# A channel mixer by block products with seven multiplications for eight, in two phases with the rows between them in DRAM

## The chip, the cores and the metric

The kernel runs on one core of one Trainium2 chip. Its engines work side by side and meet through semaphores: TensorE (PE) multiplies matrices, VectorE (DVE), ScalarE (ACT) and GpSimd (POOL) do elementwise work, SyncE (SP) issues the DMAs. The metric is the device time of one execution in microseconds; lower is better.

## The reference, cut to what matters

One layer of a hybrid backbone works on 1152 tokens of width 1024: 128 prompt tokens and 1024 latent ones. A mixer of DeltaNet and retention heads comes first, then the channel mixer, which is what the change is about:

```
h = layer_norm(x) * (1.0 + sc2) + sh2
f = einsum('btf,fd->btd', square(relu(einsum('btd,df->btf', h, w_ff1) + b_ff1)), w_ff2) + b_ff2
x = layer_norm(ALPHA * x + g2 * f, ln2_w, ln2_b)
```

`w_ff1` is 1024 x 4096, `w_ff2` 4096 x 1024, all in float32.

## The kernel before, in words

Every large product is made of three matmuls for one: a float32 operand is split into a high part, rounded to the format that TensorE multiplies in one pass (a copy on ACT, L156), and the rest (a subtraction on DVE, L157). The product is high x high, high x low and low x high, summed in PSUM. `dense` (the matmul at L190) takes one block of 128 weight columns and one chunk of 384 tokens: 8 slices of the width x 3 parts = 24 matmuls of 384 columns.

The layer runs in stages: modulation, retention heads, DeltaNet heads with the gates, output projection with the first norm (`op_load`, `op_mm`, `norm1`, `norm2`, `modulate`), channel mixer, last norm. The output projection adds two halves of the heads. `half_out` (letter R in the order DEL) makes the half of the retention heads and alpha x for tiles of 128 tokens while the DeltaNet stage ends; `op_mm` (M in the order OPS) adds the other half. Before, R0 to R5 do so for six tiles, and `op_mm` makes both halves of the other three.

The channel mixer keeps the normalised tokens in SBUF, as high and low parts (hH, hL) with the width on the partitions. For each of 32 blocks f of 128 hidden columns `ff1` makes three chunks of 24 matmuls; each chunk goes through a ReLU with its bias on ACT (L1145), a square on POOL (L1146), a copy to the high part on ACT (L1147) and the low part on DVE (L1148). `ff2` takes two blocks f at a time: for each of nine tiles and two halves of 512 output columns 6 matmuls of 512 columns (L1195), whose sum DVE adds to the accumulators `acc` in SBUF (L1199). The hidden rows never leave SBUF. First and second product alternate: 144 matmuls of `ff1`, then 108 of `ff2`. The last four blocks f are done together, with the residual (`before_last`: a product on POOL, L1217, an addition on DVE, L1218) made ahead of them, and the last norm follows tile by tile in an order written out by hand (FIN). `acc` is finished by lines L1225 to L1234.

The tile framework takes the program, orders the instructions of each engine by the order of the text (and by the numbers behind ^ in the orders), by its own estimate of when an operand is there, and by when a buffer comes free, and sets the semaphores. Each tag has a fixed number of buffers. All DMAs go through one queue, SP, in the order that it has set.

## Time and profile before

| what | us |
|---|---|
| median of 3 runs | 1662.03 |
| lowest and highest run | 1659.66 and 1662.29 |
| the profiled execution | 1663.03 |
| its span, first to last instruction | 1661.3 |
| mean granted clock of TensorE | 0.977 |

All durations quoted come from the profiled execution; its time is 1.7 us more than its span. A view that cuts the span into stretches gives the busy time of each engine in each. The groups of instructions give, for each line and shape, the busy time, the mean of one instruction in ns, and the idle time in front of them with what ended it. The chain of waits follows what ended last back to the start. The records of a matmul (PE) have a modelled end that overlaps the next one; weight loads (PEld) are listed apart.

### The profile page before, as it was taken

The numbers are of one execution on the slowest core, as the hardware profiler recorded it, in microseconds if no ns is written. First come the engines' busy times: TensorE is split into PE (matmuls) and PEld (weight loads), VectorE is DVE, ScalarE is ACT, GpSimd is POOL, SyncE is SP. The second block draws the span as 40 slices with busy tenths as digits, with TensorE's granted clock in tenths as the row PEclk, the third lists the DMA queues.
The fourth block names the chain that finished last, engine by engine and source line by source line (L and its number), as shares of the span: only waits on it lengthen the run. The fifth ranks groups of instructions, "written<-read, shape, count | busy, mean of one in ns | idle before, by whom it ended". The sixth has DMA issues, their size and how long they took to land.

```text
span 1661.3 us, 24439 instructions
## 1 busy us (share of the span) xinstructions
PE 1569.4 (94%) x9441; PEld 1389.1 (84%) x9441; DVE 911.8 (55%) x1776; ACT 586.3 (35%) x1313; POOL 322.4 (19%) x339
## 2 busy tenths in 40 slices
PE   4899999899999999997999999999999999999994
PEld 2797777898898899875888899998899998899883
DVE  4425235587877876567865433344444434444658
ACT  5512213664555554523582122211122212122233
POOL 2211111111021201026631011100011100012546
PEclk9899899999999999998999999999999999999997
DMA  9323554323122223462523111111111111112312
GB/s 337 105 64 107 175 168 127 81 75 90 39 81 52 61 62 106 139 202 95 165 62 119 37 51 51 48 42 39 33 44 51 51 39 44 33 39 77 119 60 101
DMA packets 161269, 144.18 MB, mean 87 GB/s; under 512 B 28484, under 2 KB 139441, under 8 KB 161025
## 3 DMA queue, kind: packets, MB, share of 16 engines
q1 hardware_dynamic: 161153, 142.62, 28.2%
q8 instruction: 74, 1.21, 0.3%
q14 instruction: 42, 0.34, 0.1%
HBM read 116.91 MB, written 21.48 MB: 83 GB/s over the span
## 4 chain that ended last, share of the span: by engine, by line
PE 61%; DVE 6%; POOL 3%; ACT 3%; DMA 2%; issue 2%; DVEq 0%; SPq 0%; POOLq 0%; ACTq 0%
PE mm L190 23%; PE s L1195 12%; PE c L190 7%; PE c L1195 4%; PE co L1195 4%; PE s L999 1%; PE c L898 1%; PE c L889 1%; POOL acc L1217 1%; PE c L882 1%; PE co L913 1%; DMA w2r<-in_w_ff_dram 1%; PE mm L999 1%; PE co L912 1%; DMA wor<-in_w_o_dram 1%
## 5 line engine op out<-in xcount | busy, mean ns | idle before, releaser
L190 PE MATMUL mm<-hH,wh 128*128 128x384 f32 x1176 | 408.8, 348 | 3.4 <-ACT raw L632 1.9
L190 PE MATMUL mm<-hL,wh 128*128 128x384 f32 x1176 | 407.9, 347 | 0.1
L190 PE MATMUL mm<-hH,wl 128*128 128x384 f32 x1176 | 405.7, 345 | 0.0
L190 PEld LDWEIGHTS mm<-hH,wh 128*128 128x128 f32 x1176 | 224.0, 191 | 10.0 <-issue 2.1
L190 PEld LDWEIGHTS mm<-hL,wh 128*128 128x128 f32 x1176 | 224.0, 191 | 7.0 <-issue 4.5
L190 PEld LDWEIGHTS mm<-hH,wl 128*128 128x128 f32 x1176 | 223.9, 190 | 4.9 <-issue 3.7
L1146 POOL TENSOR_TENSOR rl<-rl 128x384 f32<-128x384 f32 x96 | 83.7, 872 | 621.3 <-ACT rl L1145 621.3
L1148 DVE TENSOR_TENSOR al<-rl,ah 128x384 fp32r<-128x384 f32 x93 | 53.6, 578 | 199.5 <-ACT ah L1147 199.4
L157 DVE TENSOR_TENSOR wl<-wr,wh 128x512 fp32r<-128x512 f32 (+1 forms) x136 | 100.5, 743 | 113.8 <-ACT wh L156 112.4
L156 ACT CAST w2h<-w2r 128x1024 fp32r<-128x1024 f32 x31 | 32.5, 1049 | 302.9 <-PE s L1195 172.6
L1199 DVE TENSOR_TENSOR acc<-acc,s 128x512 f32<-128x512 f32 x141 | 96.4, 686 | 78.2 <-PE s L1195 78.2
L1195 PE MATMUL s<-w2h,ah 128*128 128x512 f32 x334 | 130.2, 390 | 3.4 <-DVE acc L1199 2.6
L1195 PE MATMUL s<-w2h,al 128*128 128x512 f32 x334 | 130.0, 389 | 0.0
L1195 PE MATMUL s<-w2l,ah 128*128 128x512 f32 x334 | 129.9, 390 | 0.0
L156 ACT CAST wh<-wr 128x512 fp32r<-128x512 f32 (+1 forms) x136 | 82.7, 613 | 120.3 <-PE mm L190 47.0
L1145 ACT ACTIVATE rl<-mm,vec 128x384 f32<-128x384 f32 x64 | 37.3, 583 | 127.8 <-PE mm L190 127.8
L190 PE MATMUL c<-hH,wh 128*128 128x384 f32 x240 | 80.9, 337 | 1.3 <-ACT hH L156 1.3
L190 PE MATMUL c<-hL,wh 128*128 128x384 f32 x240 | 81.0, 338 | 0.3 <-DVE hL L157 0.3
L190 PE MATMUL c<-hH,wl 128*128 128x384 f32 x240 | 80.9, 337 | 0.0
L1147 ACT CAST ah<-rl 128x384 fp32r<-128x384 f32 x93 | 47.8, 514 | 91.3 <-POOL rl L1146 91.3
L1195 PEld LDWEIGHTS s<-w2h,ah 128*128 128x128 f32 x334 | 62.7, 188 | 17.3 <-DVE acc L1199 3.4
L1195 PEld LDWEIGHTS s<-w2l,ah 128*128 128x128 f32 x334 | 62.7, 188 | 13.1
(385 smaller groups left out, 2990.6 us busy)
## 6 DMA issues: line engine op xcount, KB each, us to landing
wm<-in_w_mod_dram SPq DMA_DIRECT2D x32, 512.0 KB
wr<-in_w_ff_dram SPq DMA_DIRECT2D x64, 256.0 KB
w2r<-in_w_ff_dram SPq DMA_DIRECT2D x32, 512.0 KB
wr<-in_w_in_dram SPq DMA_DIRECT2D x56, 256.0 KB
wm<-in_w_mod_dram SPq DMA_DIRECT2D x8, 1024.0 KB
gr<-GR SPq DMA_DIRECT2D x24, 192.0 KB
GT<-gt SPq DMA_DIRECT2D x24, 192.0 KB
b<-X SPq DMA_DIRECT2D x9, 512.0 KB
```

What stands on the lines that cost most here:

```text
L156: S.copy(out=pool_hi, in_=src)
L157: V.tensor_tensor(out=pool_lo, in0=src, in1=pool_hi.bitcast(F32), op=ALU.subtract)
L190: T.matmul(p[:, 0:384], x[:, k % 4, :], y[c][:, k, :], start=(k == 0 and a == 0), stop=(k == 7 and a == 2),)
L882: T.matmul(p[:, 0:128], qk[:, 0, off(n):off(n) + 128], old, start=True, stop=True)
L889: T.matmul(p[:, 0:128], UP[:, m_, 0, :], r, start=True, stop=True)
L999: T.matmul(p, x[y][k], wo[k0 + k][z][:, js], start=(first and a == k == 0), stop=(last and a == 2 and k == 3))
L1145: S.activation(out=a, in_=p[:, 0:384], func=AF.Relu, bias=vec2[:, 60 + f:61 + f])
L1146: G.tensor_tensor(out=a, in0=a, in1=a, op=ALU.mult)
L1147: S.copy(out=hs, in_=a)
L1148: V.tensor_tensor(out=ls, in0=a, in1=hs.bitcast(F32), op=ALU.subtract)
L1195: T.matmul(p, x[:, ts], w[:, js], start=(i == 0 and a == 0), stop=(i == n - 1 and a == 2))
L1199: V.tensor_tensor(out=acc[t][:, js], in0=acc[t][:, js], in1=p, op=ALU.add)
```

## The change

Both products of the channel mixer are done by a scheme of block products: the operands are cut into 2 x 2 blocks, seven products of sums and differences of blocks take the place of eight, and the four blocks of the result are sums of these. The two products no longer alternate but are two phases, and the hidden rows pass through DRAM.

First product. A pair p is two blocks of 128 hidden columns; the weights are cut by width (two halves of 512) and by column block, the tokens by width and by half (`TH` = 576 tokens). A product is 2 chunks of 288 tokens x 4 slices x 3 parts = 24 matmuls of 288 columns, in `product`. The seven forms of the tokens are made once (`late_tokens`, `early_tokens`, `both_tokens`) and kept as high and low parts; the seven forms of the weights are made for each pair on POOL and split. For the first three pairs four of the seven products are made early, two while the output stage still runs (`begin_late`, J in OPS) and two behind it (`begin_early`), and their results wait in SBUF and DRAM (`HC`). ReLU and square are both on ACT now. For the first 14 pairs the rows go to DRAM in the seven forms that the second product needs (`HS`), the prompt rows beside them (`HP`); the last two pairs go as they are (`HR`).

Second product. Seven blocks of two pairs each: the seven forms of the rows are read back and split, the seven forms of the weights made on POOL and split, and for each form 4 x 6 matmuls of 512 columns go into PSUM and are added to one of seven accumulators (`mac`). The prompt tile is done with four of the same weight forms (`PROMPT`). In the last block the accumulators are joined (`after2`, `after1`, `after7`). The last four hidden blocks are done plainly, as before, after `before_last` for all nine tiles.

Also: `half_out` now makes all nine tiles (R6, R7, R8); the weights of the output projection are loaded through the two buffers `wr`; PSUM is four buffers of two banks from the output stage on (`pd`); the order of the output stage is new. The ReLU's buffers, `dense`, and the attention stages before are unchanged.

```diff
+TH = 576
+CH = 288
...
-DEL = "P0 i0 v0^1000 P1^50 m0^2500 G1 i1 G5 v1^150 b0 s0 P2 G6 b1^50 n0 t0^6000 m1 i2^150 v2 s1 P3 i3 n1 b2^1000 t1^2500 m2 G7 v3 s2^50 G0^150 G4 b3^2500 G2 m3 W^1000 n2 t2^150 s3^400 G3^50 n3^400 O^150 R0 t3^50 R1^1000 R2 R3 R4 R5"
+DEL = "P0 i0 v0^1000 P1^50 m0^2500 G1 i1 G5 v1^150 b0 s0 P2 G6 b1^50 n0 t0^6000 m1 i2^150 v2 s1 P3 i3 n1 b2^1000 t1^2500 m2 G7 v3 s2^50 G0^150 G4 b3^2500 G2 m3 W^1000 n2 t2^150 s3^400 G3^50 n3^400 O^150 R0 t3^50 R1^1000 R2 R3 R4 R5 R6 R7 R8"
+OPS = "L0 M0 L1 L2 L3 M1 A0 L4 M2 B0 A1 M3 C0 L5 B1 A2 M4 C1 L6 B2 A3 M5 C2 L7 T0 B3 A4 M6 C3 L8 B4 A5 M7 C4 T1 B5 A6 M8 C5 B6 A7 J0 C6 B7 A8 J1 C7 B8 J2 U1 C8 U0"
...
+    def pd():
+        return psum.tile([128, 1024], F32, tag="d", name="d", bufs=4)
...
+        cuts = [(1, 128 * t, 0, 128)] if t < 4 else [(2, 128 * t - TH, 0, 128)] if t > 4 else [(2, 0, 64, 64), (1, 512, 0, 64)]
+        for th, col, off_, n in cuts:
+            for k in range(8):
+                S.activation(
+                    out=qraw[f"{1 + k // 4}{th}"][:, k % 4, col:col + n],
+                    in_=p[:, 128 * k + off_:128 * k + off_ + n], func=AF.Identity,
+                    scale=modT[:, 32 + k, m:m + 1], bias=modT[:, 24 + k, m:m + 1],
+                )
...
+    def to_parts(name, q, src):
+        hi, lo = (chunk(x, q) for x in H[name])
+        S.copy(out=hi, in_=src)
+        V.tensor_tensor(out=lo, in0=src, in1=hi.bitcast(F32), op=ALU.subtract)
+    def combine(name, q, pool_, tag, bufs, u, v, op_, eng):
+        d = sb(pool_, [128, NT], tag, bufs).rearrange("p (k c) -> p k c", c=CH)
+        eng.tensor_tensor(out=d, in0=chunk(qraw[u], q), in1=chunk(qraw[v], q), op=op_)
+        return lambda: to_parts(name, q, d)
+    def late_tokens(q):
+        if "3" not in H:
+            H["3"] = htile(hpool, "hH1"), htile(hpool, "hH2")
+            H["5"] = htile(hpool, "hL2"), htile(hpool, "hL0")
+        combine("3", q, op, "d", 1, "12", "22", ALU.subtract, G)()
+        to_parts("5", q, chunk(qraw["22"], q))
+    def early_tokens(q):
+        if "4" not in H:
+            H["4"] = htile(ow, "q5"), htile(ow, "q4")
+            H["2"] = htile(oq, "q6"), htile(hpool, "hL1")
+        combine("4", q, op, "d", 1, "21", "11", ALU.subtract, V)()
+        to_parts("2", q, chunk(qraw["11"], q))
+    def both_tokens():
+        for name, u, v, op_, eng, places in (
+            ("6", "12", "11", ALU.add, V, ((fq, "z0"), (fq, "z1"))), ("7", "21", "22", ALU.add, G, ((ow, "q1"), (ow, "q3"))),
+            ("1", "22", "11", ALU.add, V, ((ow, "q0"), (ow, "q2"))),
+        ):
+            parts_ = [combine(name, q, fq, "af", 3, u, v, op_, eng) for q in (1, 0)]
+            H[name] = [htile(*z) for z in places]
+            for z in parts_:
+                z()
...
+    NP, NS = 16, 14
+    HC = [dram.tile([2, 128, TH], F32, name=f"HC{p}") for p in range(3)]
+    HS = [dram.tile([7, 128, 512], F32, name=f"HS{p}") for p in range(NS)]
+    HP = [dram.tile([128, 2, 128], F32, name=f"HP{p}") for p in range(NS)]
+    HR = {f: dram.tile([128, NT], F32, name=f"HR{f}") for f in range(2 * NS, 2 * NP)}
...
+    def product(name, w, qs=(0, 1)):
+        p = pd().rearrange("p (q c) -> p q c", q=2)[:, :, 0:CH]
+        hs = H[name]
+        for q in qs:
             for k in range(4):
+                for a, (x, y) in enumerate(((0, 0), (0, 1), (1, 0))):
+                    T.matmul(
+                        p[:, q, :], w[x][:, k, :], hs[y][:, k, CH * q:CH * q + CH],
+                        start=(k == 0 and a == 0), stop=(k == 3 and a == 2),
+                    )
+        return p
...
+    def late_products(x, y, c12, w3, w5):
+        m = product("3", w3)
+        S.copy(out=two(y), in_=m)
+        m = product("5", w5)
+        S.copy(out=two(x), in_=m)
+        G.tensor_tensor(out=c12, in0=x, in1=y, op=ALU.add)
+    def early_products(x, y, c21, w4, w2):
+        m = product("4", w4, (1, 0))
+        V.tensor_tensor(out=two(x), in0=m, in1=two(x), op=ALU.subtract)
+        S.copy(out=two(c21), in_=m)
+        m = product("2", w2, (1, 0))
+        V.tensor_tensor(out=two(y), in0=two(y), in1=m, op=ALU.subtract)
+        V.tensor_tensor(out=two(c21), in0=two(c21), in1=m, op=ALU.add)
+    def last_products(x, y, c11, c22, ws_):
+        m = product("6", ws_[0], (1, 0))
+        V.tensor_tensor(out=two(y), in0=two(y), in1=m, op=ALU.add)
+        m = product("7", ws_[1], (1, 0))
+        V.tensor_tensor(out=two(x), in0=two(x), in1=m, op=ALU.add)
+        m = product("1", ws_[2], (1, 0))
+        V.tensor_tensor(out=two(c11), in0=two(x), in1=m, op=ALU.add)
+        V.tensor_tensor(out=two(c22), in0=two(y), in1=m, op=ALU.add)
...
+    def begin_late(p):
+        a = w1_raw(p, 0, 0)
+        w3 = w_split(a)
+        b = w1_raw(p, 1, 0)
+        G.tensor_tensor(out=b, in0=b, in1=a, op=ALU.add)
+        w5 = w_split(b)
+        x, y = hold(p)
+        c12 = next_stage()
+        late_products(x, y, c12, w3, w5)
+        squared_relu(c12, 2 * p)
+        dma(HC[p][0], c12)
...
+    w1s = {}
+    def w1_load(p):
+        if p not in w1s:
+            w1s[p] = [sb(fq, [128, 4, 256], "w1", 2) for _ in range(2)]
+            for half in range(2):
+                dma(
+                    w1s[p][half],
+                    w_ff1[512 * half:512 * half + 512, 256 * p:256 * p + 256].rearrange("(k p) c -> p k c", p=128),
+                )
+        return w1s[p]
+    def pair(p):
+        f = 2 * p
+        w1 = w1_load(p)
...
+        def combined(u, v, op_, eng):
+            raw = sb(wpool, [128, 4, 128], "wr", 2)
+            eng.tensor_tensor(out=raw, in0=u, in1=v, op=op_)
+            return w_split(raw)
+        af, ag = sb(fq, [128, NT], "af", 3), sb(fq, [128, NT], "af", 3)
+        c11, c12, c21, c22 = (z[:, TH * j:TH * j + TH] for z in (af, ag) for j in range(2))
+        x, y = hold(p)
+        if p < NB:
+            dma(c12, HC[p][0])
+            dma(c21, HC[p][1])
+        else:
+            late_products(x, y, c12, w_split(p11), combined(p11, p12, ALU.add, G))
+            squared_relu(c12, f)
+            early_products(x, y, c21, w_split(p22), combined(p21, p22, ALU.add, G))
+            squared_relu(c21, f + 1)
+        last_products(x, y, c11, c22, (
+            combined(p21, p11, ALU.subtract, G), combined(p12, p22, ALU.subtract, G), combined(p11, p22, ALU.add, G),
+        ))
+        squared_relu(c11, f)
+        squared_relu(c22, f + 1)
+        if p >= NS:
+            dma(HR[f], af)
+            dma(HR[f + 1], ag)
+            return
+        a11, a21, a12, a22 = (z[:, 128 + 512 * j:640 + 512 * j] for z in (af, ag) for j in range(2))
+        dma(HP[p][:, 0, :], af[:, 0:128])
+        dma(HP[p][:, 1, :], ag[:, 0:128])
+        dma(HS[p][2], a11)
+        dma(HS[p][3], a22)
+        for name, u, v, op_, eng in (
+            (4, a11, a12, ALU.add, G), (1, a21, a22, ALU.add, V), (0, a11, a22, ALU.add, G),
+            (6, a12, a22, ALU.subtract, V), (5, a21, a11, ALU.subtract, G),
+        ):
+            s_ = next_stage()[:, 0:512]
+            eng.tensor_tensor(out=s_, in0=u, in1=v, op=op_)
+            dma(HS[p][name], s_)
...
+    close_op()
+    fq, close_fq = pool("fq")
+    w1_load(0)
+    for p in range(NB):
+        begin_early(p)
+    both_tokens()
+    for p in range(NP):
+        if p == NB:
+            XY["stage"] = XY["z"][4:]
+        pair(p)
+    close_fq()
...
+        def b_part(r, name):
+            (b11, b12), (b21, b22) = ((t[:, 0:512], t[:, 512:1024]) for t in r)
+            u, v, op_ = {
+                "3": (b12, b22, ALU.subtract), "4": (b21, b11, ALU.subtract), "1": (b11, b22, ALU.add),
+                "7": (b21, b22, ALU.add), "6": (b11, b12, ALU.add), "5": (b22, None, None), "2": (b11, None, None),
+            }[name]
+            if v is None:
+                return parts_of(u, "v", V)
+            t = sb(fp, [128, 512], "ws", 2)
+            G.tensor_tensor(out=t, in0=u, in1=v, op=op_)
+            return parts_of(t, "v", G)
...
+        PROMPT = {"3": (1, 0, True, False), "5": (1, 2, False, True), "4": (0, 1, True, False), "2": (0, 2, False, True)}
+        def block(b, after):
+            nonlocal b2
...
+            for name in "3542176":
+                x = []
+                for p, r in zip(ps, raws):
+                    a = a_part(p, name)
+                    x.append((a, b_part(r, name)))
+                if prompts is None:
+                    prompts = [prompt_part(p) for p in ps]
...
+                for tt in range(2):
+                    m = pd()
+                    for u in range(2):
+                        j = 2 * tt + u
+                        three_passes(
+                            m[:, 512 * u:512 * u + 512],
+                            [([z[:, 128 * j:128 * j + 128] for z in a], w) for a, w in x], True, True,
+                        )
+                    dst = mac[name][:, 2 * tt:2 * tt + 2, :]
+                    if b:
+                        V.tensor_tensor(out=dst, in0=dst, in1=halves(m), op=ALU.add)
+                    elif name in "34":
+                        bias = halves(b2)[:, "43".index(name), None, :].to_broadcast([128, 2, 512])
+                        V.tensor_tensor(out=dst, in0=halves(m), in1=bias, op=ALU.add)
+                    else:
+                        S.copy(out=dst, in_=halves(m))
+                if name in PROMPT:
+                    if pp is None:
+                        pp = pd()
+                    h, i, first, last = PROMPT[name]
+                    three_passes(
+                        pp[:, 512 * h:512 * h + 512], [([z[:, i, :] for z in q], w) for q, (_, w) in zip(prompts, x)],
+                        first, last,
+                    )
+                    if name == "2":
+                        V.tensor_tensor(out=pacc, in0=pp, in1=pacc if b else b2, op=ALU.add)
+                if after and name in after:
+                    after[name]()
...
+        def after2():
+            join("6", [("3", ALU.add), ("2", ALU.subtract)], (G, V))
+            join("2", [("4", ALU.add)], (V, G))
+            join("4", [("5", ALU.subtract)], (G, V))
+            join("3", [("5", ALU.add)], (V, G))
+        def after1():
+            join("4", [("1", ALU.add)], (V, G))
+            join("6", [("1", ALU.add)], (G, V))
+        def after7():
+            join("4", [("7", ALU.add)], (V, G))
+        block(NS // 2 - 1, {"2": after2, "1": after1, "7": after7})
...
+        def last_ff2(t):
+            j, c = (2, 0) if t == 0 else divmod(t - 1, 4)
+            p = pd()
+            for h in range(2):
+                js = slice(512 * h, 512 * h + 512)
+                three_passes(
+                    p[:, js], [([z[:, 128 * c:128 * c + 128] for z in acts[f][j]], ws[f][h]) for f in fs], True, True
+                )
+                u = sb(fp, [128, 512], "u", 2)
+                V.tensor_tensor(out=u, in0=p[:, js], in1=g2[min(t, 1)][:, js], op=ALU.mult)
+                V.tensor_tensor(out=acc[t][:, js], in0=u, in1=acc[t][:, js], op=ALU.add)
...
```

358 lines of the change are left out of this document (192 added, 166 removed).

## The prediction

> **What bounds the kernel now.** I read the page's table of engines first, then the busy time of each engine in stretches cut at the changes of work, then the chain of waits for the pace of one matmul, then the groups of instructions in two of these stretches for what the helpers cost.
>
> ```profile
> span 1661.3 us, 24439 instructions
> ...
> PE 1569.4 (94%) x9441; PEld 1389.1 (84%) x9441; DVE 911.8 (55%) x1776; ACT 586.3 (35%) x1313; POOL 322.4 (19%) x339
> ```
> ```profile
> 718.00:755.00 37.00, 37.00 (x160) 29.83 (x159) 25.39 (x36) 7.55 (x14) 8.70 (x6) 1.00 0.49 157
> 755.00:790.00 35.00, 23.44 (x94) 18.87 (x93) 29.28 (x56) 14.64 (x27) 23.88 (x24) 0.85 0.32 106
> 790.00:832.00 42.00, 42.00 (x201) 34.62 (x200) 36.93 (x68) 24.13 (x42) 25.60 (x27) 1.00 0.49 160
> 832.00:885.00 53.00, 48.60 (x262) 45.06 (x261) 30.81 (x50) 38.15 (x81) 15.82 (x17) 0.97 0.32 102
> 885.00:1519.00 634.00, 634.00 (x3234) 580.23 (x3233) 266.12 (x386) 137.11 (x230) 64.01 (x77) 1.00 0.15 45
> 1519.00:1567.00 48.00, 44.79 (x222) 39.46 (x220) 28.53 (x31) 5.99 (x10) 25.34 (x12) 1.00 0.34 110
> ...
> 1588.00:1638.00 50.00, 49.91 (x219) 40.68 (x217) 33.58 (x43) 21.78 (x37) 26.96 (x25) 1.00 0.12 49
> 1638.00:1661.30 23.30, 0.00 (x0) 0.00 (x0) 19.71 (x32) 3.50 (x3) 13.68 (x13) 0.61 0.30 121
> ```
>
> Each row is a stretch, its length, then busy time (and instructions) of PE, weight loads, DVE, ACT and POOL, the granted clock, the DMA share and GB/s. The mixer MLP runs from about 832 to 1638. In its steady part PE is busy for 634.00 of 634.00 us at clock 1.00, while DVE is at 42%, ACT at 22% and POOL at 10%. So every matmul less is time less there, and the helpers have room. Since ends of matmuls are modelled, I take the price of one from starts, in the chain:
>
> ```profile
> 1208.62 4.16 PE c L190 x24
> ...
> 1229.34 4.08 PE s L1195 x18
> ```
>
> A matmul of 384 columns costs 4.16/24 = 173.3 ns, one of 512 costs 4.08/18 = 226.7 ns. The line through both has 0.4167 ns a column and 13.3 ns fixed.
>
> **The products.** Before, the first product has 32 column blocks x 3 chunks x 24 = 2304 matmuls of 384: 399.4 us. After, it has 16 pairs x 7 products x 2 chunks x 12 = 2688 matmuls of 288. The trace has no such width; on the line one costs 133.3 ns, 358.4 in all, so 41.0 are saved. Bounds: 120 ns without the fixed part (322.6) and 173.3 ns if narrower buys nothing (465.9). How short a load-and-multiply step can be is shown by nine transposes, 128 columns wide with a 128-column load each:
>
> ```profile
> 470.75 1.20 PE L650 MATMUL s<-ident,qk 128*128 128x128 f32 x9 [0.19 <-ACT qk L640]
> 470.75 0.96 PEld L650 LDWEIGHTS s<-ident,qk 128*128 128x128 f32 x9 [0.51 <-ACT qk L640]
> ```
>
> Nine matmuls took 1.20 us, 133 ns a step with the last one's own tail in it, and nine loads 0.96 us, 107 a step. This is the nearest row to 288 columns, and in it loading is no slower than 133 ns, so I take the line. The Trainium skill (TensorE: Matmul & The Clock Gate, section Back-to-back issue gap) gives columns over 2.4 plus 2.5 ns for a warm stream; by it 288 columns would be 122.5 ns and the first product 329 us, but at 384 it says 162.5 where this trace has 173.3, so the trace decides.
>
> The second product has 32 x 9 x 2 x 3 = 1728 matmuls of 512, 391.7 us. After: 7 blocks x 7 products x 24 = 1176, with 7 x 24 = 168 for the prompt rows and 4 x 9 x 6 = 216 plain ones, 1560 in all, 353.6 us. That saves 38.1. Together 79.1 us leave PE.
>
> **Head of the change.** The stretch from 718 to 885 is not PE-bound, and here the change adds work for the helpers.
>
> ```profile
> L241 DVE BATCH_NORM_STATS2 lnst<-hL 128x6 f32<-128x512 f32 x24 | 15.8, 675 | 4.2 <-POOL hL L1092 2.8 <-POOL hL L1082 1.3
> L1092 POOL TENSOR_TENSOR hL<-hL,l1b 128x1024 f32<-128x1024 f32 x6 | 15.2, 2527 | 5.8 <-DVE hL L1091 5.8
> L1082 POOL TENSOR_TENSOR hL<-hL,gx 128x512 f32<-128x512 f32 x6 | 8.3, 1391 | 3.2 <-DVE gx L1080 3.2
> L1091 DVE TENSOR_TENSOR hL<-hL,l1w 128x1024 f32<-128x1024 f32 x6 | 7.7, 1281 | 4.1 <-ACT hL L251 4.1
> L992 POOL TENSOR_TENSOR wr<-wr 128x512 f32<-128x512 f32 x4 | 7.0, 1747 | 5.8 <-DMA wr<-OT 5.8
> L1082 DVE TENSOR_TENSOR hL<-hL,gx 128x512 f32<-128x512 f32 x6 | 6.3, 1056 | 0.1
> L1080 DVE TENSOR_TENSOR gx<-s,g 128x512 f32<-128x512 f32 x9 | 6.1, 672 | 0.0
> ```
> ```profile
> L157 DVE TENSOR_TENSOR wl<-wr,wh 128x512 fp32r<-128x512 f32 x50 | 34.6, 692 | 34.0 <-ACT wh L156 34.0
> L157 DVE TENSOR_TENSOR w2l<-w2r,w2h 128x1024 fp32r<-128x1024 f32 x27 | 33.0, 1221 | 5.2 <-ACT w2h L156 5.2
> L156 ACT CAST wh<-wr 128x512 fp32r<-128x512 f32 x50 | 31.0, 619 | 35.7 <-PE c L190 35.7
> L1199 DVE TENSOR_TENSOR acc<-acc,co 128x512 f32<-128x512 f32 x44 | 30.2, 687 | 26.3 <-PE co L1195 26.3
> L1145 ACT ACTIVATE rl<-mm,vec 128x384 f32<-128x384 f32 x52 | 30.3, 582 | 118.1 <-PE mm L190 118.1
> ```
>
> The first fence is from 718 to 832, where POOL is busy too, the second from the steady part; the figure behind the comma is one instruction in ns. An addition of 512 in SBUF costs DVE 1056 ns beside POOL and a like subtraction 692 ns without it; readings from PSUM (672, 687) don't change.
>
> Three half outputs (R6 to R8) move ahead of the others' second halves: 72 matmuls, nine DMAs of tokens and heads (three times 256 + 256 + 512 KB), three POOL products. On SP they pass ahead of the last output weights and the norm's rows, at a DMA share of 0.49; they fill the hole of 11.6 us that PE has between 755 and 790. I cost them at nothing: the same work, done in a hole. If the early weights came late instead, the 72 matmuls (16.3 us) would only wait elsewhere.
>
> Then nine tiles pass, each with two PSUM products, an addition, four statistics, one row product and one split on DVE: 2 x 0.672 + 1.056 + 4 x 0.675 + 1.281 + 0.692 = 7.1 us, 64 in all. New on DVE are ten operations of 1152 (forms 3, 5, 4, 2): 1221 x 1152/1024 = 1.37 us each, 13.7; and six weight splits, 4.2. That is 82 us against PE's 216 x 0.2267 + 72 x 0.133 + 144 x 0.1333 = 77.8. With 15 us for the first tile's way through and the operations under 0.3 us that I left out, the stage takes 97, which is 19 of PE idle. Behind it the three early halves take PE 19.2 us and DVE 6 + 4 operations of 1152 (13.7), nine PSUM operations of 576 (0.687 x 576/512 = 0.77, 7.0) and six splits (4.2): 25, so 6 idle. The first three pairs are short, 72 matmuls or 9.6 us, beside six POOL operations at about 1.5 (9.0 us) and 3.5 MB of DMA.
>
> ```profile
> GB/s 62 379 410 419 240 114 388 408 411 406 415 406 410 407 403 273 83 0 0 0 129 84 0 0 0 0 105 198 384 181 117 359 159 0 0 0 7 0 0 104
> 869.69 5.20 DMA w2r<-in_w_ff_dram
> ```
>
> The row is the first 100 us, where loads alone filled the DMA engines: 410 GB/s, so 8.5 us a pair. Three resources at the same load, and a weight buffer of one pair only: I take 7 idle for the three. Head: 32 idle against 11.6 + 4.4 = 16.0 by the table, some 18 with the small gaps that modelled ends hide; **14 more**, between -10 (the old idle time goes, nothing comes) and 40 (each part twice as long).
>
> **Other pairs.** PE needs 168 x 0.1333 = 22.4 us a pair. POOL has eight operations of 512 (1.4 to 1.75) and one of 576: 13 to 16. DVE has seven PSUM operations of 576 (5.4), seven splits and two additions (0.69 to 1.06): 12 to 15. ACT has seven casts of 0.62, and three PSUM copies and eight passes of 576, at most 582 x 1.5 = 0.87 each: 14. Traffic is 2.9 MB, 130 GB/s. All lies beside PE. A write of rows waits on SP for its sum on POOL or DVE, and the next pair's weights may stand behind it; their landing (5.20 us in the chain row above) has most of 22 us, as the last use of the old weights is a sum that POOL can make two products early. Bounds 0 and 30; I take **4**.
>
> **Between the phases** the first block needs 2 MB of weights and its rows split. Its buffers lie on those of forms 3, 5 and 2, which are free three products (9.6 us) before the end; loading takes 5 at 410 GB/s, combining and splitting about 4. Bounds 0 and 15; **5**.
>
> **Blocks.** PE needs 192 x 0.2267 = 43.5 us. POOL has ten sums and ten subtractions of 512: 28 to 35. DVE has 18 subtractions (0.69 to 1.06) and 14 PSUM accumulations of 1024, each between 1.22 and 1.37, with three smaller: 32 to 41. ACT has 28 casts: 17.3, and 1 for the prompt. DMA 6 MB, 138 GB/s. Near, but inside PE's time, with three products of prefetch. Bounds 0 and 60 in the seven; **6**.
>
> **The end.** All nine of these now stand between the last block and the final rows:
>
> ```profile
> L1217 POOL TENSOR_TENSOR acc<-acc,g 128x1024 f32<-128x1024 f32 x9 | 22.3, 2497 | 13.8 <-DVE acc L1199 10.2 <-DMA g<-GD 3.6
> L1218 DVE SCALAR_TENSOR_TENSOR acc<-b,acc 128x1024 f32<-128x1024 f32 x9 | 17.6, 1959 | 16.6 <-DMA b<-X 10.3 <-POOL acc L1217 6.2
> 1642.78 0.69 DVE acc L1225
> 1644.07 1.68 DVE acc L1225
> ```
>
> DVE was busy for 33.6 + 19.7 = 53.3 of the last 73.3 us; 17.6 more make 71, and PE's last part is 49. The 3.2 us that PE lost from 1519 to 1567 go. Net **4**, between -3 and 12.
>
> **Sum.** 14 + 4 + 5 + 6 + 4 = 33 against 79.1: 46 less. The profiled execution took 1663.0 us, 1.7 over its span, and lies 1.0 above the median of the runs. Forecast 1617.
>
> **Rivals.** *Weight loading is the floor.* The steady row has 580 us of weight loads in 634, and a load is recorded at 188 ns where 133 are wanted:
>
> ```profile
> L190 PEld LDWEIGHTS mm<-hH,wl 128*128 128x128 f32 x416 | 78.1, 188 | 0.0
> ```
>
> If the step cannot fall below 173 ns, 2688 of them cost 465.9, 107.5 over my term: 1725, slower. It decides from 133.3 + 46/2.688 = 150 ns on. Against it: records of 188 follow each other every 173, so they overlap, the nine transposes stepped faster, and 512 against 384 columns differ by the full streaming time. The Trainium skill (Trainium Kernel Development and Optimization, section Performance Expectations) names the busy share of weight loads, not of matmuls, as the measure of TensorE; by it PE stands at 92% of a limit that counts loads, and the loads rise from 4032 to 4248. *DVE beside POOL becomes the bound of the blocks.* The last two rows above are one operation alone and beside POOL: 0.69 and 1.68. With all 18 subtractions at 1.68 a block's DVE work is 30 + 19 + 3 = 52, 8.5 over PE, 60 in seven: 1677, slower. It decides from 43.5 + 46/7 = 50 us, a mean of 1.56. Against it: where both engines worked, the mean was 1.06. *Handing over costs more*: rows or weights land late, or a cast queues behind a copy that waits, about 1.6 us in each of the 16 pairs and 7 blocks, 37 us: 1654. For it: 60 MB more traffic and one queue, SP, for all; against: the low shares. *No loss beyond the old ones*: 79.1 less some 5, 1589; the change would then simply do what it says.
>
> **Chances.** Forecast 0.60 (1600 to 1636), handing over 0.16 (1637 to 1665; 0.02 of it within 0.2%, 0.01 slower), no loss 0.13, loading 0.06, DVE 0.05. About 0.2%, 3.3 us, is what can be told from no change. Faster: 0.60 + 0.13 + 0.13 = 0.86; same 0.02; slower 0.12. The range 1590 to 1653 leaves out half of the no-loss case, part of handing over and the two slow rivals, some 0.2.
>
> **What would show it.** Right: starts of 288-column matmuls 133 ns apart; PE full in pairs 3 to 15 at about 22.4 us each and in blocks at 43.5; PE idle most ahead of pair 3. Wrong: a step of 150 ns or more; blocks near 50 us with DVE or POOL full; PE waiting at DMA for rows; a head or tail more than 20 us longer.

## The result, and the profile after

The changed kernel takes 1725.17 us (median of 4 runs, 1724.13 to 1726.13) against 1660.85 for the kernel before on the same chip (1659.08 to 1662.29): a ratio of 1.0388, 95% interval 1.037 to 1.0406. It is slower by 64 us; the forecast was 46 less. The profiled execution has a span of 1722.5 us, 61.2 over that of before.

The page's first lines, in the columns shown for before:

```profile
span 1722.5 us, 26166 instructions
...
PE 1528.1 (89%) x9657; PEld 1337.6 (78%) x9657; DVE 1127.2 (65%) x1854; ACT 740.4 (43%) x1557; POOL 701.2 (41%) x554
```

By its records TensorE is busy for 41 us less (matmuls at a slow clock count longer in them) and stands still for about 100 us longer; POOL has more than twice its work. The same stretches view as before, cut where the stages change:

```profile
716.00:869.00 153.00, 119.79 (x481) 92.96 (x479) 93.94 (x155) 50.48 (x91) 67.87 (x60) 0.89 0.42 134
869.00:1029.00 160.00, 124.32 (x849) 120.91 (x848) 93.30 (x118) 79.23 (x131) 78.36 (x57) 0.90 0.39 130
1029.00:1279.00 250.00, 248.67 (x1872) 248.43 (x1872) 157.59 (x179) 124.43 (x201) 140.91 (x95) 1.00 0.37 129
1279.00:1295.00 16.00, 0.00 (x0) 0.00 (x0) 0.54 (x1) 3.87 (x7) 4.54 (x4) 0.56 0.84 313
...
1300.00:1588.00 288.00, 288.00 (x1261) 238.22 (x1262) 239.03 (x229) 123.33 (x216) 204.60 (x148) 0.99 0.50 157
1588.00:1611.00 23.00, 19.80 (x80) 15.87 (x80) 20.68 (x13) 6.93 (x14) 22.92 (x9) 0.93 0.04 11
1611.00:1709.00 98.00, 62.90 (x218) 46.25 (x216) 82.83 (x83) 26.11 (x42) 63.17 (x44) 0.79 0.23 78
1709.00:1722.50 13.50, 0.00 (x0) 0.00 (x0) 9.72 (x16) 1.24 (x1) 6.69 (x7) 0.57 0.29 117
```

In order: output projection; early halves and pairs 0 to 4; pairs 5 to 15; the hole between the phases; blocks; end of the last block; final product; tail. The third and fifth rows are what the change is for, and there it does what it promised: TensorE full, clock 1.00 and 0.99. The chain of waits gives the price of a matmul, for the second product from the second block to the sixth:

```profile
1029.41 248.68 PE d L1194 x1872
...
1344.79 217.37 PE d L1404 x959
```

248.68/1872 = 132.8 ns for 288 columns (133.3 forecast) and 217.37/959 = 226.7 for 512, as before. At these prices the two products are 2688 x 0.1328 + 1560 x 0.2267 = 711 us where they were 791. Everything that went wrong lies in the other rows.

To place it I took, from the timeline of TensorE, the first start and last end of the matmuls of each stage (us). "Last block" is the end of the 1344th matmul of the second product; 216 are left then, 49 us at 226.7 ns.

| kernel | output projection | first product | second product | last block | end |
|---|---|---|---|---|---|
| before | 702-829 | both, 831-1638 | | | 1661.3 |
| after | 716-869 | 870-1278 | 1295-1709 | 1611 | 1722.5 |
| e2 | 714-867 | 868-1276 | 1284-1698 | 1599 | 1710.6 |
| e3 | 718-873 | 873-1274 | 1291-1706 | 1605 | 1719.1 |
| e4 | 728-881 | 927-1295 | 1313-1727 | 1627 | 1739.7 |
| e5 | 716-870 | 871-1273 | 1290-1706 | 1605 | 1717.9 |
| e6 | 719-875 | 876-1287 | 1304-1718 | 1619 | 1730.8 |
| e7 | 720-873 | 874-1281 | 1298-1705 | 1609 | 1716.9 |
| e8 | 719-873 | 874-1283 | 1299-1676 | 1615 | 1719.5 |
| e9 | 697-855 | 856-1264 | 1281-1695 | 1595 | 1708.3 |
| e10 | 715-869 | 869-1277 | 1293-1722 | 1621 | 1734.5 |
| e12 | 702-860 | 861-1263 | 1271-1652 | 1599 | 1693.2 |
| e13 | 700-858 | 859-1261 | 1269-1636 | 1579 | 1685.2 |
| e14 | 722-875 | 876-1282 | 1299-1690 | 1615 | 1704.8 |
| e15 | 714-867 | 868-1274 | 1291-1685 | 1606 | 1697.4 |
| e16 | 717-872 | 873-1280 | 1296-1673 | 1606 | 1685.4 |
| e17 | 714-860 | 865-1276 | 1293-1682 | 1608 | 1718.9 |
| e18 | 700-847 | 852-1256 | 1265-1646 | 1574 | 1683.6 |

The difference of the spans, step by step: the output projection starts 14 later; it takes 153 for 127 (26 more); from there to the last matmul 840 for 809 (31 more); the tail is 13 for 23 (10 less). 14 + 26 + 31 - 10 = 61. The 840 hold 711 of products and 129 lost, in which waits and matmuls at a slow clock stand together: 52 from the projection's end to the end of the first product, 17 between the phases, 60 in the second product (6 in the first block, 5 in the last, 49 in the final product). The 809 of before held 791 and lost 18, some 13 ahead of 885 and 5 from 1519 on. So 80 us were saved on TensorE, and 14 + 26 + 129 - 18 - 10 = 141 were put in.

The 52 of the first product lie ahead of pair 5. The stretches view of its line alone, cut at the first matmuls of the first early half made behind the output stage (913.4), of pair 0 (938.4), of pair 3 (972.1), of pair 4 (1005.6) and of pair 5 (1032.7); the figures are busy PE and PEld, clock, DMA share and GB/s:

```profile
870.00:913.40 43.40, 20.89 (x145) 20.28 (x145) 0.87 0.22 76
913.40:938.40 25.00, 22.06 (x144) 21.24 (x145) 0.89 0.31 96
938.40:972.10 33.70, 30.73 (x218) 30.27 (x217) 0.95 0.56 182
972.10:1005.60 33.50, 25.25 (x170) 24.61 (x169) 0.90 0.47 159
1005.60:1032.70 27.10, 24.37 (x171) 23.91 (x170) 0.94 0.43 153
```

Against 144, 144, 216, 168 and 168 matmuls at 132.8 ns, they lose 24, 6, 5, 11 and 5 us; 1 more lies ahead of the first matmul. From pair 5 on nothing is lost.

### The profile page after: what moved, and what is told of

It is laid out like the page before. It is cut to its first block, busy times and chain, and to the rows that moved or that the text cites. A ratio compares the mean times of both kernels' runs of the same rounds, so it can differ in the third digit from the quotient of the medians.

```text
span 1722.5 us, 26166 instructions
## 1 busy us (share of the span) xinstructions
PE 1528.1 (89%) x9657; PEld 1337.6 (78%) x9657; DVE 1127.2 (65%) x1854; ACT 740.4 (43%) x1557; POOL 701.2 (41%) x554
## 4 chain that ended last, share of the span: by engine, by line
PE 48%; POOL 8%; DVE 8%; DMA 5%; ACT 4%; issue 4%; SPq 0%; POOLq 0%; DVEq 0%; ACTq 0%
PE d L1404 17%; PE d L1194 15%; PE mm L192 7%; PE d L999 2%; DMA wr<-OT 1%; DVE wl L159 1%; DMA w<-in_w_ff_dram 1%; POOL mrow L1522 1%; PE c L898 1%; DVE lnst L243 1%; PE c L882 1%; POOL wr L992 1%; PE c L889 1%; PE co L913 1%; POOL hL L1106 1%
## 5 line engine op out<-in xcount | busy, mean ns | idle before, releaser
L192 PE MATMUL mm<-hH,wh 128*128 128x384 f32 x672 | 238.9, 356 | 1.8 <-ACT raw L632 1.8
L192 PE MATMUL mm<-hL,wh 128*128 128x384 f32 x672 | 237.5, 353 | 0.0
L192 PE MATMUL mm<-hH,wl 128*128 128x384 f32 x672 | 236.0, 352 | 0.0
L1404 PE MATMUL d<-vh,sh 128*128 128x512 f32 x456 | 183.4, 403 | 37.5 <-ACT sh L1369 17.3
L1194 PE MATMUL d<-q,wh 128*128 128x288 f32 x896 | 197.2, 302 | 17.2 <-ACT wh L158 9.6
L1404 PE MATMUL d<-vh,sl 128*128 128x512 f32 x456 | 183.4, 402 | 10.5 <-DVE sl L1370 10.5
L1404 PE MATMUL d<-vl,sh 128*128 128x512 f32 x456 | 181.8, 400 | 0.0
L1194 PEld LDWEIGHTS d<-q,wh 128*128 128x128 f32 x896 | 151.8, 194 | 18.4 <-ACT wh L158 11.1
L1194 PE MATMUL d<-q,wl 128*128 128x288 f32 x512 | 153.6, 300 | 4.0 <-DVE wl L159 4.0
L1370 DVE TENSOR_TENSOR sl<-ar,sh 128x512 fp32r<-128x512 f32 x106 | 119.4, 1144 | 45.0 <-ACT sh L1369 45.0
L1404 PEld LDWEIGHTS d<-vh,sh 128*128 128x128 f32 x456 | 88.8, 195 | 59.6 <-ACT sh L1369 17.6
```

The lines of the kernel that those rows point to most:

```text
L192: T.matmul(p[:, 0:384], x[:, k % 4, :], y[c][:, k, :], start=(k == 0 and a == 0), stop=(k == 7 and a == 2),)
L1194: T.matmul(p[:, q, :], w[x][:, k, :], hs[y][:, k, CH * q:CH * q + CH], start=(k == 0 and a == 0), stop=(k == 3 and a == 2),)
L1370: eng.tensor_tensor(out=lo, in0=src, in1=hi.bitcast(F32), op=ALU.subtract)
L1404: T.matmul(p, x, w, start=(first and i == a == 0), stop=(last and i == n - 1 and a == 2))
```

## The experiments

Each was made against the changed kernel; a time stands beside 1725.17, a ratio beside 1.0388. Intervals are 0.2 to 0.5% to each side, and the changed kernel was timed beside other runs of the kernel before, so a difference under some 8 us is read only where a stage of the table moved with it.

**e1, the residual tile by tile in the last product.** My first theory for the end was that POOL's nine products with the gate stand in front of the low parts of the last weights.

```diff
-        for t in range(9):
-            before_last(t)
         def last_ff2(t):
+            before_last(t)
```

> The residual of the last norm is added tile by tile behind each tile's final matmuls, not for all nine tiles ahead of them; the operations are the same. Theory: POOL's nine products of 1024 (2.5 to 2.8 us) and the joins stand in its queue ahead of the low parts of the last weights, and PE waits for these from 1604 to 1642; with the products behind, PE's hole shrinks and the whole is 15 to 30 us shorter than the changed kernel. Rival: DVE and POOL are full there with work that must be done anyway; then within 5 us.

1726.38, ratio 1.0385 (1.0343 to 1.0427). The text moved, the instructions did not: on POOL the framework put the products in the same order as before. This tells nothing of the theory.

**e2, rows of the last pairs through ACT's queue.** SP's queue in the hole, from the timeline of the changed kernel:

```profile
1258.66 23.18 SPq L84 DMA_DIRECT2D HR<-af  x4
1281.93 3.03 SPq L84 DMA_DIRECT2D w2a<-in_w_ff_dram  x4
```

The second entry begins when the first ends (1258.66 + 23.18 = 1281.84). The writes of the last pair's rows wait for the rows' last squares, and the weights of the second product, which need nothing of them, stand behind for 23 us.

```diff
-            dma(HR[f], af)
-            dma(HR[f + 1], ag)
+            nc.scalar.dma_start(out=HR[f], in_=af)
+            nc.scalar.dma_start(out=HR[f + 1], in_=ag)
```

> The plain rows of the last two pairs are written to DRAM from ACT's DMA queue, not from SP's. Theory: between the phases the loads of the second product stand behind these writes on SP, which wait for the last pair's results; PE's hole of 21 us goes down to 6 to 12, and the whole is 8 to 15 us shorter than the changed kernel. Rival: the loads wait for buffers of the first phase, or the first block's sums are slow by themselves; then within 3 us.

1716.43, ratio 1.0328 (1.0287 to 1.037): 9 less. The hole shrank from 17 to 8 us (1276 to 1284). Shown: half of the hole was the order of one queue.

**e3, without the last three forms of the tokens.**

```diff
-    both_tokens()
+    H.update({"6": H["3"], "7": H["4"], "1": H["5"]})
```

> Left out: the three token forms 6, 7 and 1, for which forms 3, 4 and 5 are multiplied in their place; so 12 sums and splits of 1152 elements are gone and all matmuls stay. Theory: the elementwise work of the forms is on the path behind the output stage; 15 to 25 us shorter than the changed kernel. Rival: the short pairs wait for weight loads and for the writes of rows, beside which the forms are made; then 0 to 6 us.

1721.31, ratio 1.0353 (1.0316 to 1.039): 4 less, and the first product takes 401 for 408. All the work on DVE, POOL and ACT for these forms is worth some 7 us, so it does not make the 52 lost in the first product.

**e4, without early halves.** `NB = 0`, and J0, J1 and J2 taken out of OPS.

> No pair is begun early: all 16 pairs make their seven products in one go, nothing of them runs in the output stage, and the way through DRAM of the first three is gone. Theory: the short pairs cost more than their early halves fill, as a pair of 9.6 us of matmuls has one buffer of weights that takes 3.5 to 6.6 us to land and rows to write; 10 to 30 us shorter than the changed kernel. Rival: the early halves fill holes of the output stage, and without them their 38 us of matmuls come on top; 10 to 25 us longer.

1736.2, ratio 1.0449 (1.0407 to 1.0491): 11 more. Of the 17 us by which its profiled execution is the longer one, 12 lie ahead of the projection, where nothing of this edit runs; from the projection's end to the end of the first product it takes 414 us for 409. The stretches view of e4, output projection and what follows it:

```profile
728.00:881.00 153.00, 120.59 (x483) 93.21 (x481) 86.09 (x152) 48.07 (x87) 63.06 (x57) 0.89 0.39 125
881.00:927.00 46.00, 7.20 (x34) 5.56 (x32) 28.58 (x41) 26.61 (x47) 16.62 (x16) 0.56 0.16 58
```

Without the halves TensorE does 7.20 us in 46 while the last norms and the forms are made, and no engine is full. That is a latency, and the halves hide a part of it. They bring back most of what they hide: without them the first pair loses 11 us and no later one anything, where the changed kernel loses 27 behind 913.4. Its early halves are worth some 5 us.

**e5, more stage buffers in the short pairs.** They have one buffer for five sums that go to DRAM; the waits view of the changed kernel from 869 to 1029 has:

```profile
DVE xy L1333 <- DMA HS<-xy: 15.8, 5, 5.9
...
POOL xy L1333 <- DMA HS<-xy: 11.0, 3, 4.6
```

```diff
+        if p < NB:
+            XY["stage"] = XY["z"][:2 * p + 2] + XY["z"][6:]
         squared_relu(c11, f)
```

> In the three short pairs the five sums of rows go through three, five and seven buffers on their way to DRAM in place of one: the pair's own two and those of the pairs before it, which are done with. Theory: with one buffer each sum waits for the write before it (1.3 us on POOL, 2.0 to 3.5 us to land), 15 to 18 us a pair against 9.6 us of matmuls; 10 to 25 us shorter than the changed kernel. Rival: the pair's one buffer of weights sets the pace; then 0 to 5 us.

1720.12, ratio 1.0361 (1.0344 to 1.0378): 5 less, the first product 402 for 408. Pair 4 now takes 22.3 us for 27.1. Most of the 26.8 us of waits were beside the path.

**e6, the three moved halves inside the output stage.** R6, R7 and R8 leave the end of DEL; OPS gets them behind L1, A0 and A1, and their sums get the PSUM buffers of that stage.

```diff
-OPS = "L0 M0 L1 L2 L3 M1 A0 L4 M2 B0 A1 M3 C0 ..."
+OPS = "L0 M0 L1 R6 L2 L3 M1 A0 R7 L4 M2 B0 A1 R8 M3 C0 ..."
```

> The half outputs R6, R7 and R8 stand behind the first, second and third tile of the output stage and not in the stage before. Theory: the output stage is a chain of about 12 us a tile whatever PE has to do, so the 72 matmuls (16.3 us) with their loads fill its holes, while ahead of it they lengthen the stage before; 10 to 20 us shorter than the changed kernel. Rival: it is the loads and sums of these tiles, not their place, that cost; then within 5 us, or longer.

1729.77, ratio 1.0413 (1.0391 to 1.0435): 5 more. My theory that only their place was wrong fell: the first product with the gate comes 50 us after the projection's start for 64, the last one 160 after it for 157; the projection is 156 long for 153 and the first product 411 for 408. Likely their loads and sums delay the tiles there as well; no run shows that by itself.

**e7, the end's elementwise work on DVE alone.** Joins, low parts of the last weights and the residual's product, which alternated between POOL and DVE or were POOL's, all on DVE.

```diff
-                    engines[(tt + x) % 2].tensor_tensor(out=u, in0=u, in1=v, op=op_)
+                    V.tensor_tensor(out=u, in0=u, in1=v, op=op_)
...
-            ws[f] = [parts_of(r[:, 512 * j:512 * j + 512], "v", G if j else V) for j in range(2)]
+            ws[f] = [parts_of(r[:, 512 * j:512 * j + 512], "v", V) for j in range(2)]
...
-            G.tensor_tensor(out=acc[t], in0=acc[t], in1=g2[m], op=ALU.mult)
+            V.tensor_tensor(out=acc[t], in0=acc[t], in1=g2[m], op=ALU.mult)
```

> From the last block on, the joins, the low parts of the last weights and the residual's product are all on DVE, none on POOL; 22 operations more for DVE. Theory: beside POOL a DVE operation of two SBUF operands takes 1.7 to 2.3 us where it takes 0.7 to 1.2 alone, so two engines do no more than one; the end gets 5 to 20 us shorter, and the joins of 1024 take 1.2 us each. Rival: the two engines share the work; with DVE alone the end is 15 to 30 us longer.

1718.78, ratio 1.0348 (1.0332 to 1.0363): 6 less. The last block takes 44 us for 49, the final product 95 for 98. One engine did the work of two in no more time. The groups from 1588 to 1660 say why; of the changed kernel:

```profile
L1370 DVE TENSOR_TENSOR sl<-ar,sh 128x512 fp32r<-128x512 f32 x8 | 19.2, 2429 | 0.0
L1471 DVE TENSOR_TENSOR mrow<-mrow,m 128x1024 f32<-128x1024 f32 x4 | 8.0, 2023 | 2.3 <-POOL mrow L1471 2.3
```

and of e7:

```profile
L1471 DVE TENSOR_TENSOR mrow<-mrow,m 128x1024 f32<-128x1024 f32 x8 | 9.4, 1223 | 0.0
L1370 DVE TENSOR_TENSOR sl<-ar,sh 128x512 fp32r<-128x512 f32 x10 | 6.6, 695 | 0.0
```

The same subtraction of 512 takes DVE 2429 ns beside a busy POOL (56.58 of the 72 us) and 695 beside an idle one (7.86), a join 2023 and 1223.

**e8, the residual behind the product.** `before_last` goes; the last product is added to the accumulator as it is (DVE, from PSUM), then multiplied (POOL for six tiles, DVE for three), then added to the residual.

```diff
-        for t in range(9):
-            before_last(t)
...
-                V.tensor_tensor(out=u, in0=p[:, js], in1=g2[min(t, 1)][:, js], op=ALU.mult)
-                V.tensor_tensor(out=acc[t][:, js], in0=u, in1=acc[t][:, js], op=ALU.add)
+            V.tensor_tensor(out=acc[t], in0=p, in1=acc[t], op=ALU.add)
+            (G if t < 6 else V).tensor_tensor(out=acc[t], in0=acc[t], in1=g2[m], op=ALU.mult)
+            V.scalar_tensor_tensor(out=acc[t], in0=x1, scalar=ALPHA, in1=acc[t], op0=ALU.mult, op1=ALU.add)
```

> The final sum is one addition of PSUM of 1024 to the accumulator, then the product with the gate (POOL for tiles 0 to 5, DVE for 6 to 8), then the residual: so the nine products cannot run ahead of the last weights' low parts, and DVE has 1.4 us a tile less. Theory: POOL's nine products were in front of the low parts for which PE waits; 15 to 30 us shorter than the changed kernel. Rival: the joins and splits alone fill both engines until 1640; then 0 to 8 us.

1716.29, ratio 1.0338 (1.0316 to 1.0359): 9 less. Final product and tail of e8:

```profile
1615.00:1676.00 61.00, 54.47 (x217) 43.00 (x216) 31.35 (x33) 14.81 (x24) 35.16 (x25) 0.92 0.22 73
1676.00:1719.00 43.00, 0.00 (x0) 0.00 (x0) 34.24 (x43) 12.48 (x20) 25.51 (x22) 0.55 0.30 111
```

TensorE is done 61 us after the last block instead of 98, and then the tail is 43 instead of 13. The hole moved behind the matmuls.

**e9, a buffer of their own for the output weights.** The change loads them through `wr`, the two buffers in which the tokens are multiplied too.

```diff
-            raw = flat(sb(wpool, [128, 4, 128], "wr", 2))
+            raw = sb(oq if k in (2, 3) else ow, [128, 512], "wor", 1)
```

> The raw output weights have one buffer of their own again, as before the change, and don't share the two through which the heads' rows come. Theory: the first half output starts 14 us later than before (716 against 702) and the nine take 7.5 us each, not 6, because weights and rows queue for the same two buffers; 8 to 20 us shorter than the changed kernel. Rival: DMA time or POOL sets the pace there; then within 4 us.

1712.37, ratio 1.0309 (1.0269 to 1.0349): 13 less, the projection starts at 697 instead of 716. It is 158 long for 153. Shown: the late start is this buffer; this run and the three versions below that have its edit start at 697 to 702, all others at 714 to 728.

**e10, joins spread over three blocks.** `move` joins an accumulator in block 3, 4 or 5, after which each of its products is added to every accumulator that needs it, up to ten additions from PSUM more in a block.

```diff
-                        V.tensor_tensor(out=dst, in0=dst, in1=halves(m), op=ALU.add)
+                        for n_, op_ in dests[name]:
+                            dst = mac[n_][:, 2 * tt:2 * tt + 2, :]
+                            V.tensor_tensor(out=dst, in0=dst, in1=halves(m), op=op_)
...
-        block(NS // 2 - 1, {"2": after2, "1": after1, "7": after7})
+        for b in range(NS // 2):
+            block(b, {3: {"2": in3}, 4: {"5": in4}, 5: {"1": in5_1, "7": in5_7}}.get(b))
```

> The accumulators are joined in blocks 3, 4 and 5 in place of the last one, and from then on a product is added to both of its blocks straight from PSUM: 24 more additions on DVE in all over the last three blocks, no join in the last. Theory: the joins are the backlog that holds POOL and DVE at the end, beside PE's hole of some 38 us; the blocks get a few us slower, the end 20 to 30 faster: 12 to 28 us shorter than the changed kernel. Rival: the low parts of the last rows and the residual fill the end anyway, or the blocks become DVE-bound; then within 6 us.

1734.83, ratio 1.0437 (1.04 to 1.0474): 10 more. The last block of e10:

```profile
1570.00:1621.00 51.00, 44.56 (x192) 35.47 (x192) 51.00 (x47) 15.28 (x29) 32.57 (x19) 1.00 0.32 99
```

DVE is busy for 51.00 of 51 us, 6 more than TensorE: the rival "DVE becomes the bound of the blocks", which the changed kernel escapes with DVE busy for 239 of 288 us, appears as soon as DVE gets more. The last four blocks take 45 to 50 us each. The final product still took 101: the joins were gone from it, but their work was on DVE as additions, and DVE came to the end of the blocks without a pause. A subtraction of 512 still took it 1742 ns there.

**e11 and e12, several edits together:** e2 + e5 + e8 + e10, and in e12 e9 too.

> Together: rows of the last pairs written from ACT's queue, more buffers for the sums of the short pairs, joins in blocks 3 to 5, final sum ahead of the residual. By the theory of separate losses 9 + 5 + 9 and the joins' 12 to 28 add up: 1675 to 1695 us. Rival: the end's two changes free the same time; 1695 to 1705.

> As the one before, and the raw output weights with a buffer of their own. If the shared buffers hold the output stage, 8 to 20 us below the one before, so 1660 to 1685; if not, the same.

1709.9, ratio 1.0278 (1.0237 to 1.0318), and 1694.99, ratio 1.0203 (1.0165 to 1.0241). Both lie above the ranges that I had given, which still counted on a gain by e10. The 15 between them repeat what e9 gave.

**e14, e15, e16, what the end is made of.** e14 leaves out the joins, e15 the residual, e16 both.

```diff
-        block(NS // 2 - 1, {"2": after2, "1": after1, "7": after7})
+        block(NS // 2 - 1, None)
```
```diff
-        for t in range(9):
-            before_last(t)
+        for m in range(2):
+            g2[m] = row("w2a", 4, GD[2 + m:3 + m, :])
```

> Leaves out the sixteen additions of 1024 that join the accumulators, so part of the computation, and nothing else. In the changed kernel they take DVE about 12 and POOL 17.6 us between 1587 and 1621. Theory, that the end is a backlog of elementwise work on these two engines and the joins stand first in it: 12 to 18 us less, the final 216 matmuls in about 83 us for 98. Rival, that the last matmuls are held by the residual, whatever stands ahead of it: under 5 us less.

> Leaves out the residual of the last norm (nine products with the gate on POOL, nine additions on DVE), so part of the computation, and nothing else. They take POOL some 24 and DVE some 13 us between 1601 and 1662. Theory, a backlog in which every elementwise operation counts: 13 to 24 us less. Rival, that the residual is the whole of the end's loss: the final 216 matmuls take 52 to 60 us for 98 and the tail stays at 13, so 38 or more less. Second rival, low parts of the last weights and rows hold the matmuls: under 5.

> Leaves out both the joins and the residual, so part of the computation. If the two are a backlog on the same engines, the gains of the two runs add up, 30 to 40 us less in all, and the final 216 matmuls take under 60 us. If they stand side by side on different engines, this gains more than the two together.

1705.95, 1701.88 and 1686.41 (ratios 1.0278, 1.0267 and 1.0175, each within 0.0052): 19, 23 and 39 less. Final product and tail, of e14, e15 and e16:

```profile
1615.00:1690.00 75.00, 56.41 (x217) 42.98 (x215) 59.03 (x71) 24.77 (x40) 46.60 (x36) 0.91 0.19 69
1690.00:1704.80 14.80, 0.00 (x0) 0.00 (x0) 9.51 (x16) 1.24 (x1) 8.40 (x7) 0.59 0.26 106
```
```profile
1606.00:1685.00 79.00, 60.86 (x218) 45.57 (x216) 55.88 (x76) 26.22 (x42) 41.82 (x36) 0.85 0.14 50
1685.00:1697.40 12.40, 0.00 (x0) 0.00 (x0) 8.20 (x15) 1.24 (x1) 4.76 (x5) 0.64 0.32 127
```
```profile
1606.00:1673.00 67.00, 55.64 (x218) 43.10 (x216) 45.09 (x62) 25.09 (x41) 36.24 (x33) 0.90 0.12 47
1673.00:1685.40 12.40, 0.00 (x0) 0.00 (x0) 8.59 (x15) 1.24 (x1) 4.75 (x5) 0.63 0.32 127
```

From 98 the final product falls to 75, 79 and 67, the tail stays at 12 to 15, and the gains in time add up (19 + 23 against 39). No single operation holds TensorE; a queue of elementwise work on DVE and POOL does, joins first, then low parts and residual. The joins take POOL 22.9 us and DVE 15.7, the residual 24.5 and 15.3: the gain was about what the busier of the two was relieved of, not the sum.

**e17, both halves multiplied before either is read.** In the projection TensorE's waits were mostly for the gate's products, and at the end many for `u`. Both read one half of a buffer of two banks while the other is still to be multiplied, and the framework might order by whole buffers.

```diff
             out_mm(p[:, js], x, 0, js, True, True)
+        for j in range(2):
+            js = slice(512 * j, 512 * j + 512)
             V.tensor_tensor(out=y[:, js], in0=p[:, js], in1=g1[min(t, 1)][:, js], op=ALU.mult)
...
+            for h in range(2):
+                js = slice(512 * h, 512 * h + 512)
                 u = sb(fp, [128, 512], "u", 2)
```

> One buffer of two banks now holds both halves of a tile's product, in the output projection and in the final product, and the text of the program reads the first half before it multiplies the second. New theory: the program orders by whole buffers, so the second half's matmuls wait for VectorE's reading of the first (27.0 us of TensorE's waits in the output projection behind the products with the gate, 13.2 at the end behind the products u). Here both halves are multiplied first and read then, in both places, nothing else. By this theory the output projection's 153 us shrink by 15 to 27, the final 216 matmuls' 98 by 5 to 13, in all 20 to 40 us less. Rival, that these waits only mark a DVE that is late anyway: under 5 us in all, the waits showing up before another matmul.

1720.65, ratio 1.035 (1.0326 to 1.0375): 5 less. The waits view of the projection, after and e17:

```profile
PE d L999 <- DVE gx L1097: 27.0, 8, 5.5
```
```profile
PE d L1125 <- ACT n L253: 24.8, 6, 7.2
```

The waits for the gate went, as the theory had it, and 24.8 us of waits for the norm came in their place, before the transposes. The projection took 146 us for 153, but the first early half behind it came 195 us after the projection's start for 198; the final product took 74 for 98, and the tail 37 for 13. So the false dependency is real and nearly free: in both places the elementwise chain is late anyway.

**e13 and e18, the best versions.** e13 joins e2, e5, e8, e9 and the first two edits of e7. e18 has the two loops of e17 and the residual ahead again, in place of e8.

> All edits that helped by themselves, without the one that cost 10 us: rows of the last pairs through ACT's queue (-9), stage buffers (-5), output weights in a buffer of their own (-13), residual behind the product (-9), joins and low parts of the last weights on DVE alone (-6). Theory that the losses stand at separate places and add up: -42, about 1683 us. Rival, that two of them are the same time at the end (the residual and the joins share POOL's queue): about 1690. In either case slower than the kernel before, 1661.

> The same order of halves, with the edits that helped: rows of the last pairs through ACT's queue, stage buffers, output weights in a buffer of their own, joins and low parts of the last weights on DVE; the residual stands ahead of the final product again, its products on POOL. If the order of the halves gives 20 to 40 us and the rest adds up as before (-37 with the residual behind): 1650 to 1675, about the kernel before. If the rival holds: 1688 to 1700.

1688.25, ratio 1.0169 (1.0128 to 1.0209), and 1684.7, ratio 1.0126 (1.0103 to 1.015). e13's gains added up less than fully (37 of 42); e18 came between the two times that I had given. No version that I ran beats the kernel before; the best is 1.3% slower.

## Why the prediction was wrong, point by point

Each term of the sum, as the stages of the profiled executions have it (us; the products and the other terms together make the difference):

| term | forecast | measured |
|---|---|---|
| products | -79 | -80 |
| head, up to pair 3 | 14 | 63 |
| other pairs | 4 | 16 |
| between the phases | 5 | 17 |
| blocks | 6 | 11 |
| the end | 4 | 34 |
| sum | -46 | 61 |

**The products: right.** 132.8 ns a step for 133.3; 80 us saved for 79.1. The rival "weight loading is the floor" gave 1725, which is the measured time, and was still wrong: weight loads are recorded busy for 248.43 of 250 us in the third row, and the step is 17.2 ns shorter than the 150 from which that rival decides. The agreement of its time is luck. By the Trainium skill (Trainium Kernel Development and Optimization, section Performance Expectations), which names the busy share of weight loads among its measures of how near a kernel is to the limit, that stretch would stand at 99% of one; yet the step fell from 173.3 to 132.8 ns at the same number of loads a matmul, so no run here bears out such a limit down to this step.

**Blocks, and pairs 5 to 15: right.** Pairs 5 to 15 take 168 x 0.1328 = 22.3 us each, the second to sixth block 192 x 0.2267 = 43.5, without a stop; the blocks' 11 stand in the first and the last. The "4" for the other pairs is 16, all of it in pairs 3 and 4 (33.5 and 27.1 us). The chain of waits there runs through the short pairs' sums and their writes to DRAM; e5 takes away the share of pair 4, and in e4, which has no short pairs, neither stop is there.

**The failed step: "Head: 14 more".** 63 came: 14 before the projection starts, 26 in it, 23 behind it (36 lost up to pair 3 where some 13 were lost before). Three parts of it failed. "On SP they pass ahead ... I cost them at nothing": the hole from 755 to 790 was no free place. The timeline of DVE has the first and the last product with the gate; before:

```profile
750.77 0.68 DVE L1080 TENSOR_TENSOR gx<-s,g 128x512 f32<-128x512 f32 x1
...
835.65 0.68 DVE L1080 TENSOR_TENSOR r<-s,g 128x512 f32<-128x512 f32 x1
```

and after:

```profile
779.54 0.69 DVE L1097 TENSOR_TENSOR gx<-d,g 128x512 f32<-128x512 f32 x1
...
872.82 0.68 DVE L1097 TENSOR_TENSOR gx<-d,g 128x512 f32<-128x512 f32 x1
```

The first tile came 29 us later, 14 of them the start of the projection and 15 about the 72 matmuls (72 x 0.2267 = 16.3). Nine tiles take 85 us before, where three of them have twice the matmuls of the others, and 93 after, where none has: the work taken out of the last three tiles did not shorten the passage of the nine. That the place ahead of the first tile is to blame is not shown, as e6 gave the halves another one and won nothing. Of the 26 us, e17 takes 7 away by the order in which the new PSUM buffers of two banks are read.

The second part is the weights in `wr`, which make the 14 before the projection: the change's list named the two buffers, and I gave them no cost; e9, with a buffer of their own, takes 13 us less. The third is the length of the stage, taken as 97 us from busy times of which I had taken the largest. From the first product with the gate to the first early half behind the stage it is 134 us (779.5 to 913.4), in which TensorE is busy for 88 and DVE and POOL for 83 each, and in e4, where TensorE has none of the late halves to do, 134 again (793.1 to 927.3). Counted from the projection's start it is 198, and 195 to 202 in e4, e6, e9 and e17, whatever they moved in it. So no engine is full in it, and work taken out of it does not shorten it: a chain through the tiles sets it (matmuls, sum, norm, row products, second norm, transposes, forms). Which link counts, the matmuls at a granted clock of 0.86 among them, is not settled. The two pieces behind it were right: 6 and 5 us lost for the 6 and 7 of the sum.

**"Between the phases 5": 17.** Loads and splits were priced, the queue was not: I wrote that the buffers are free three products early, and did not ask what SP does then. e2 gave 9 of it.

**The failed step at the end: "Net 4, between -3 and 12".** It was 34: 49 lost in the final product, less 10 of the tail and 5 that the old end had lost. I had added the residual's 17.6 us to DVE beside the old tail, and had left out that the joins, the low parts and POOL's 22.3 us now fall in the same stretch, at prices that rise while both engines work: 2429 ns for 695. I had weighed just this slowing for the blocks, where it did not decide (group mean 1033 there, below the 1560 from which that rival wins), and not for the end, where it did. e14 to e16 show the backlog, e7 the price.

**What followed from it.** The three terms between the dense parts had upper bounds of 40, 15 and 12 us; 63, 17 and 34 came, all on the same side, since each took overlap for granted in a stretch where a chain or a queue runs. The range's upper end, 1653, left no room for that. The sign that I had set for this came: head and tail each more than 20 us longer.

## What to carry to other kernels

Saved matmul time counts only in the stretches in which TensorE is full; cut the trace there, and price the stretches at the ends by the chain of one tile and by its queues, not by the sum of busy times. A change that takes work from TensorE and hands sums to two elementwise engines can pay at its ends, where nothing covers them: count what must be done there in one row, at the prices that both engines show when both are busy. And before a new buffer or load is called free, look at what stands behind it on its queue and who shares its tag.
